# Both feed-forwards of an encoder layer by one level of Strassen's scheme

## The chip, the cores and the metric

The kernel runs on one core of a Trainium2 chip. What counts is the time of one launch on the device in microseconds, the median of several runs. PE is TensorE (matmuls), DVE is VectorE, ACT is ScalarE, POOL is GpSimd, SP is the engine whose queue issues most DMAs here.

## The reference

One layer of a bidirectional encoder on 512 tokens of width 1024, all in float32. The feed-forward width is 2816.

```
x = x + 0.5 * swiglu(rms_norm(x, ffn1_norm), w_gate1, w_up1, w_down1)
proj = rms_norm(x, mix_norm) @ w_in            # 1024 -> 2304
oa = differential attention, 8 heads, relative bias;  ob = grouped-query attention, rotary
x = x + concat(oa, ob) @ w_out                 # 1024 -> 1024
x = x + 0.5 * swiglu(rms_norm(x, ffn2_norm), w_gate2, w_up2, w_down2)
return rms_norm(x, final_norm)

swiglu(x, g, u, d) = (silu(x @ g) * (x @ u)) @ d
rms_norm(x, g)     = x * rsqrt(mean(x * x) + 1e-6) * g
```

## The kernel before

Every float32 matrix is held as two parts: a high part, the value cast to the type that PE takes (fp32r), and a low part, the value less the high part. A product is three matmuls, high by high, high by low and low by high (`mm3`, lines 180 to 183). ACT makes the high part (line 108), DVE then subtracts it from the raw value (line 109); both inputs of that subtraction lie in SBUF.

The weights come as blocks of up to 1 MB in a fixed list (`specs`). `Blocks.get` (line 116) hands out block i and has the conversion of block i + 1 and the load of block i + 2 written ahead of the products, at a higher priority. There are two raw buffers, two for high and two for low parts. All loads go through SP's queue.

x is kept transposed, features by tokens, as eight tiles `xT` of 128 by 512. `gained` (line 270) multiplies by the norm's gain and splits; the norm's factor of each token, R, is applied to the results of the products instead (lines 311 and 321). `stats` sums squares, on POOL for both feed-forwards (line 242), and `finish_stats` makes R from the sum.

`gate_up` (line 298) walks over 11 pairs of weight blocks of 256 hidden features, one of the gate and one of up. Each block makes two PSUM banks, each 8 x 3 matmuls of 512 columns (tokens), with the weights stationary. DVE multiplies by R, ACT applies silu, DVE multiplies gate by up, and the result is split into high and low again (`gT`). The first down projection (lines 402 to 417) has four passes of 256 output features, each over 22 groups of 128 hidden features, 512 tokens wide; the second (lines 920 to 942) has tokens in the rows and two passes of 512 output features.

Attention and the projections lie between; their order is set by loops over (head, 128 tokens) units with projection work filled in. The order on each engine is made by a scheduler when the program is built, from the order of writing, priorities and a model of times. The weights' conversions, the evacuations of PSUM and the splits share DVE's and ACT's queues, and each engine works its queue in order.

Of the kernel before, what the change touches and what calls it, by code (L numbers as in the profile page):

```python
# [17 lines left out]
P = 128  # L18
S = 512
# [8 lines left out]
POOL_ACC = ("f1", "f2")  # L28
SQ = 1
# [4 lines left out]
PX = "BBC"  # L34
UP = "DD"
DN1 = ("BB", "DD")
DN2 = ("AADD", "BBBC")
# [4 lines left out]
LAG_V = 4  # L42

# [31 lines left out]
class Blocks:  # L75


    def __init__(self, tc, pool, specs, ahead):
        self.tc, self.nc, self.pool, self.specs, self.ahead = tc, tc.nc, pool, specs, ahead
        self.raw, self.split = {}, {}  # L80
        self.nload = self.nsplit = 0

    def load(self, upto):
        while self.nload < min(upto, len(self.specs)):
            i = self.nload
            name, src, n, w, parts = self.specs[i]
            t = self.pool.tile([P, n, w], F32, tag="raw", name=f"raw_{name}", bufs=2)
            step = (n + parts - 1) // parts
            for a in range(0, n, step):
                b = min(n, a + step)  # L90
                for c0, c1, s in src:
                    self.nc.sync.dma_start(out=t[:, a:b, c0:c1], in_=s[:, a:b, :])
            self.raw[i] = t
            self.nload += 1

    def convert(self, upto):
        while self.nsplit < min(upto, len(self.specs)):
            i = self.nsplit
# [26 lines left out]
def build(ctx, tc, a, out):  # L125
# [13 lines left out]
    wpool = ctx.enter_context(tc.tile_pool(name="wpool", bufs=2))  # L139
    psum = ctx.enter_context(tc.tile_pool(name="psum", bufs=1, space=PS))  # L140
# [56 lines left out]
    gp = tc.tile_pool(name="ffn1", bufs=1)  # L197
    fpool = gp.__enter__()
# [759 lines left out]
```

## Time and profile before

| what | value |
|---|---|
| median of 3 runs | 1023.11 us (1021.55 to 1024.03) |
| the profiled execution | 1023.65 us, span 1021.8 us |
| mean granted TensorE clock | 0.993 |
| PE busy | 1001.2 us (98%), 4963 matmuls |
| DVE busy | 540.5 us (53%) |
| ACT busy | 395.5 us (39%) |
| POOL busy | 120.3 us (12%) |
| DMA | 105.21 MB, 103 GB/s on the mean |

The span runs from the first to the last instruction. Busy time of PE is modelled from overlapping matmuls, so a busy PE is not PE at its peak; the distance between starts tells what a matmul costs. "Idle before" is the time in which an engine stood still ahead of an instruction, and the name behind the arrow is what ended it. Times in the stages are microseconds from the span's start.

### The profile page before, as it was taken

The page shows a single profiled execution, that of the slowest core. Times are in us where ns is not written, and L with a number is a line of the kernel's source. Part 1 is how long each engine was busy: PE and PEld are TensorE (multiplying, and loading weights), DVE is VectorE, ACT ScalarE, POOL GpSimd, SP SyncE. Part 2 cuts the span into 40 slices and gives each one's busy share as a digit, 9 for nine tenths or more (in the row PEclk, how much of TensorE's full clock was granted, in tenths as well). Part 3 has the DMA queues.
Part 4 walks back from the last instruction along what each step waited for, and adds up shares of the span by engine and source line. Part 5 has one row for each costly group of instructions (what it writes and reads, how often), then busy time and mean ns, then how long its engine had stood idle before and what let it go on. Part 6 is the DMA issues. An engine that isn't in the chain of part 4 may idle for free.

```text
span 1021.8 us, 12710 instructions
## 1 busy us (share of the span) xinstructions
PE 1001.2 (98%) x4963; PEld 843.5 (83%) x4963; DVE 540.5 (53%) x898; ACT 395.5 (39%) x668; POOL 120.3 (12%) x147
## 2 busy tenths in 40 slices
PE   8999999999999999999998999999999999999997
PEld 6788888888888889899987887888888888888885
DVE  4464454444234344768996896754454444441413
ACT  6342232232223233566776565632322322311312
POOL 2100000000000000123564344400000000000000
PEclk9999999999999999999998999999999999999999
DMA  8463223223232344544322130223224223322212
GB/s 243 155 202 120 87 83 120 87 85 112 83 113 73 113 130 120 159 133 125 112 71 62 37 98 12 83 84 123 83 84 122 83 88 119 103 83 101 85 62 82
DMA packets 94224, 105.21 MB, mean 103 GB/s; under 512 B 4716, under 2 KB 78980, under 8 KB 94164
## 3 DMA queue, kind: packets, MB, share of 16 engines
q1 hardware_dynamic: 93588, 103.35, 32.8%
q8 instruction: 39, 0.64, 0.3%
q10 hardware_dynamic: 576, 1.05, 0.3%
q14 instruction: 21, 0.17, 0.1%
HBM read 93.86 MB, written 6.32 MB: 98 GB/s over the span
## 4 chain that ended last, share of the span: by engine, by line
PE 92%; DVE 3%; issue 2%; ACT 1%; DMA 1%; POOL 1%; SPq 0%; POOLq 0%; ACTq 0%; DVEq 0%
PE g L182 8%; PE g L181 8%; PE u L181 8%; PE g L183 8%; PE u L183 8%; PE u L182 8%; PE dn L183 8%; PE dn L182 8%; PE dn L181 8%; PE poA L544 2%; PE pqk L182 1%; PE pqk L181 1%; PE pqk L183 1%; PE po L181 1%; PE po L183 1%
## 5 line engine op out<-in xcount | busy, mean ns | idle before, releaser
L108 ACT CAST hi_b<-raw_b 128x1024 fp32r<-128x1024 f32 (+1 forms) x162 | 158.9, 1029 | 326.6 <-PE dn L183 82.3
L109 DVE TENSOR_TENSOR lo_b<-raw_b,hi_b 128x1024 fp32r<-128x1024 f32 (+1 forms) x162 | 192.1, 1222 | 163.0 <-ACT hi_b L108 162.8
L182 PE MATMUL g<-xl_f,hi_b 128*128 128x512 f32 x352 | 137.7, 392 | 0.0
L181 PE MATMUL u<-xh_f,hi_b 128*128 128x512 f32 x352 | 137.2, 390 | 0.0
L183 PE MATMUL g<-xh_f,lo_b 128*128 128x512 f32 x352 | 137.1, 390 | 0.0
L182 PE MATMUL u<-xl_f,hi_b 128*128 128x512 f32 x352 | 137.0, 389 | 0.0
L181 PE MATMUL g<-xh_f,hi_b 128*128 128x512 f32 x352 | 136.9, 392 | 0.0
L183 PE MATMUL u<-xh_f,lo_b 128*128 128x512 f32 x352 | 136.9, 389 | 0.0
L311 DVE TENSOR_TENSOR g<-g,R_f 128x512 f32<-128x512 f32 x44 | 30.2, 690 | 109.1 <-PE g L183 105.6
L321 DVE TENSOR_TENSOR u<-u,R_f 128x512 f32<-128x512 f32 x44 | 30.2, 690 | 91.6 <-PE u L183 91.6
L182 PEld LDWEIGHTS g<-xl_f,hi_b 128*128 128x128 f32 x352 | 66.4, 189 | 13.9 <-issue 0.2
L181 PEld LDWEIGHTS g<-xh_f,hi_b 128*128 128x128 f32 x352 | 66.3, 189 | 13.8
L183 PEld LDWEIGHTS u<-xh_f,lo_b 128*128 128x128 f32 x352 | 66.1, 188 | 14.1 <-issue 0.5
L183 PEld LDWEIGHTS g<-xh_f,lo_b 128*128 128x128 f32 x352 | 66.4, 189 | 13.6
L181 PEld LDWEIGHTS u<-xh_f,hi_b 128*128 128x128 f32 x352 | 66.1, 188 | 13.9 <-issue 0.2
L182 PEld LDWEIGHTS u<-xl_f,hi_b 128*128 128x128 f32 x352 | 66.1, 188 | 13.6
L593 ACT ACTIVATE s_A<-s_A,m_A 128x512 f32<-128x512 f32 x64 | 46.4, 726 | 30.5 <-DVE m_A L591 27.1
L312 ACT ACTIVATE g<-g 128x512 f32<-128x512 f32 x44 | 27.6, 630 | 69.4 <-DVE g L311 69.2
L591 DVE CUSTOM_DVE_ANT_0 s_A<-sA,T 128x512 f32<-128x512 f32 x64 | 43.7, 684 | 11.1 <-PE sA L589 10.1
L283 ACT CAST gT_0h<-u 128x512 fp32r<-128x512 f32 x22 | 13.7, 621 | 90.5 <-DVE u L322 90.5
L911 POOL TENSOR_TENSOR fr<-fr,mhalf 128x1 f32<-128x1 f32 x4 | 2.2, 556 | 347.1 <-DVE fr L910 347.1
L255 POOL TENSOR_TENSOR r_mx<-r_mx,mhalf 128x4 f32<-128x4 f32 x1 | 1.0, 1017 | 347.4 <-DVE r_mx L254 347.4
(273 smaller groups left out, 1976.1 us busy)
## 6 DMA issues: line engine op xcount, KB each, us to landing
raw_b<-ffn_w_up SPq DMA_DIRECT2D x22, 1024.0 KB, 5.4
raw_b<-ffn_w_gate SPq DMA_DIRECT2D x21, 1024.0 KB, 5.4
raw_b<-ffn_w_down SPq DMA_DIRECT2D x18, 1024.0 KB, 5.1
raw_b<-w_in SPq DMA_DIRECT2D x5, 1024.0 KB
toep<-nbd SPq DMA_DIRECT2D x8, 512.0 KB, 10.8
raw_b<-w_in SPq DMA_DIRECT2D x8, 512.0 KB, 4.6
raw_b<-w_out SPq DMA_DIRECT2D x4, 1024.0 KB, 5.2
T<-toep SPq DMA_DIRECT2D x8, 448.0 KB, 3.4
```

The lines of the kernel that those rows point to most:

```text
L108: self.nc.scalar.copy(out=hi[:, a:b, :], in_=t[:, a:b, :])
L109: self.nc.vector.tensor_sub(lo[:, a:b, :], t[:, a:b, :], hi[:, a:b, :].bitcast(F32))
L181: nc.tensor.matmul(ps, lh, rh, start=start, stop=False)
L182: nc.tensor.matmul(ps, lh, rl, start=False, stop=False)
L183: nc.tensor.matmul(ps, ll, rh, start=False, stop=stop)
L283: nc.scalar.copy(out=hi, in_=src)
L311: nc.vector.tensor_mul(g1, ps, R)
L312: nc.scalar.activation(g1, g1, AF.Silu)
L321: nc.vector.tensor_mul(u, ps, R)
L544: nc.tensor.matmul(ps, pt_sb[:, P * j:P * j + P], v(j), start=j == 0, stop=j == NT - 1)
L591: nc.vector.tensor_tensor_reduce(out=sc, in0=ps, in1=T[:, 384 - P * qt:896 - P * qt], scale=1.0, scalar=BIG, op0=ALU.add, op1=ALU.min, acc ...
L593: nc.scalar.activation(sc, sc, AF.Exp, bias=m[:, s:s + 1], scale=-1.0, accum_out=l1[:, qt, h:h + 1] if s == 0 else l2)
```

## The change

Each of the three products of a feed-forward is cut into 2 by 2 blocks and done with seven block products instead of eight (Winograd's form of Strassen's scheme). The blocks of the operands are added and subtracted first, and the results are put together from seven products:

- left operand: S1 = A21 + A22, S2 = S1 - A11, S3 = A11 - A21, S4 = A12 - S2
- right operand: T1 = B12 - B11, T2 = B22 - T1, T3 = B22 - B12, T4 = B21 - T2 (up to the sign)
- products: A11 B11, A12 B21, S4 B22, A22 T4, S1 T1, S2 T2, S3 T3

For gate and up the left operand is x: its token halves by its feature halves, made once for a feed-forward, from the normed x. The right operand is a weight block of 1024 by 256: POOL makes T1 to T4, ACT and DVE split all seven operands, and PE does 7 x 4 x 3 matmuls of 256 columns, half of the tokens. DVE adds the products up out of PSUM, silu follows, and H = 0.5 * silu(gate) * up stays in float32, unsplit. For down, hidden values are the left operand, 11 steps of 256 hidden features; PSUM has no room for seven accumulators, so there are three passes over H: four products at a time ("da"), then two ("db"), then one ("dc"), with 24, 12 and 6 matmuls of 512 columns a step. POOL makes the differences of the weights and of H.

x is kept natural, tokens by features (`xn`), and the norm is applied ahead of the products: squares on ACT, the root on POOL, one multiplication by factor and gain on DVE, then transposes. So R, `stats` and `finish_stats` go. The output projection is turned accordingly. Norm and transposes of tokens 256 to 511 after the first feed-forward are written ahead of the pass dc, those of tokens 0 to 255 behind it.

The diff, cut to its core:

```diff
+    def parts(self, hi, lo, src):
+        self.nc.scalar.copy(out=hi, in_=src)
+        self.nc.vector.tensor_sub(lo, src, hi.bitcast(F32))
...
+    def gate_up(self, t, shape, name):
+        sub = self.nc.gpsimd.tensor_sub
+        b11, b12, b21, b22 = t[:, 0:4, 0:P], t[:, 0:4, P:], t[:, 4:8, 0:P], t[:, 4:8, P:]
+        hi, lo = self.pair(shape, name)
+        T = {}
+        for n, x, y in ((3, b22, b12), (1, b12, b11), (2, b22, b12), (4, b21, None)):
+            if n != 1:
+                T[n] = self.fpool.tile([P, 4, P], F32, tag="T", name=f"T{n}_{name}", bufs=3)
+            sub(b12 if n == 1 else T[n], x, T[2] if n == 4 else y)
...
+        self.parts(hi[:, 4:8, :], lo[:, 4:8, :], t[:, 4:8, :])
+        self.parts(hi[:, 0:4, :], lo[:, 0:4, :], t[:, 0:4, :])
+        for p, n in ((7, 3), (6, 2), (4, 4)):
+            h, l = (self.fpool.tile([P, 4, P], F32R, tag=f"t{w}", name=f"t{w}{n}_{name}", bufs=4) for w in "hl")
+            self.parts(h, l, T[n])
...
+    def down_a(self, t, shape, name):
...
+        sub(T3, t[:, 2, :], t[:, 1, :])
+        self.nc.vector.tensor_sub(t[:, 1, :], t[:, 1, :], t[:, 0, :])
+        sub(T2, t[:, 2, :], t[:, 1, :])
+        self.parts(hi[:, 0:2, :], lo[:, 0:2, :], t[:, 0:2, :])
+        self.parts(hi[:, 3, :], lo[:, 3, :], T3)
+        self.parts(hi[:, 2, :], lo[:, 2, :], T2)
...
+    def down_b(self, t, shape, name):
...
+            self.nc.gpsimd.tensor_sub(T4, t[:, e, :], T2)
+            self.parts(hi[:, shape[0] + e, :], lo[:, shape[0] + e, :], T4)
...
+    def normed(t, G, tag):
...
+        for h in range(2):
+            squares(ss, z, t, h)
+        r = rsqrt(ss, f"{tag}{t}")
+        nc.vector.scalar_tensor_tensor(out=z, in0=xn[t], scalar=r, in1=G, op0=ALU.mult, op1=ALU.mult)
...
+    def one_block(i, j, m, L, Hj, g1, n):
...
+            for k in range(4):
+                mm3(ps, wh[:, k, :], wl[:, k, :], xh[:, k, :], xl[:, k, :], start=k == 0, stop=k == 3)
...
+        nc.vector.tensor_add(dst[:, 0::3, :], b_, p1.to_broadcast([P, 2, 256]))
...
+        nc.vector.tensor_add(dst[:, 1:3, :], c_, dst[:, 3:4, :].to_broadcast([P, 2, 256]))
+        nc.vector.tensor_add(dst[:, 3, :], c_[:, 0, :], dst[:, 2, :])
...
+        nc.vector.tensor_add(dst[:, 1:3, :], d_, dst[:, 1:3, :])
+        if m == "g":
+            nc.scalar.activation(g1, g1, AF.Silu)
         else:
...
+            nc.vector.scalar_tensor_tensor(out=Hj, in0=dst, scalar=0.5, in1=g1, op0=ALU.mult, op1=ALU.mult)
...
+        def left_a(j):
+            h = H[j]
...
+                nc.gpsimd.tensor_add(S13[:, 0, :], h[:, 2, :], h[:, 3, :])
+                nc.gpsimd.tensor_sub(S13[:, 1, :], h[:, 0, :], h[:, 2, :])
+                nc.gpsimd.tensor_sub(h[:, 2, :], S13[:, 0, :], h[:, 0, :])
+                parts(hl, slice(0, 1), h[:, 0:1, :])
+                parts(hl, slice(1, 2), h[:, 2:3, :])
+                parts(hl, slice(2, 4), S13)
...
+        get_a = ahead(left_a)
+        for j in range(NJ):
+            wh, wl = blocks.get(at[("da", i, j)])
+            hl = get_a(j)
+            for c, l, w in (("a", 0, 0), ("d", 3, 3), ("c", 2, 1), ("b", 1, 2)):
+                product(c, [x_[:, l, :] for x_ in hl], wh[:, w, :], wl[:, w, :], j == 0, j == NJ - 1)
...
+            nc.gpsimd.tensor_add(lo[:, :512], lo[:, :512], p1[:, e, :])
+            nc.gpsimd.tensor_add(hi[:, :512], hi[:, :512], u3[:, e, :])
```

`left_b` splits the other two quarters of H, 512 wide; `left_c` has POOL subtract two quarters, 256 wide, and splits the result; `ahead` has step j + 1 written with step j.

What stands in a row now, at three places. First DVE in gate/up of the first feed-forward: `g1` and `u` are the results of gate and up, `gT` the hidden values, `lo_b` a weight's low part, here for one gate and one up block before:

```order
L311 TENSOR_TENSOR g1_0_5_0_1057<-g0_5_0_1032,R_f1_375 128x512
L311 TENSOR_TENSOR g1_0_5_1_1085<-g0_5_1_1060,R_f1_375 128x512
L109 TENSOR_TENSOR lo_b12_1089<-raw_b12_1030,hi_b12_1088 128x1024 x2
L321 TENSOR_TENSOR u_0_5_0_1121<-u0_5_0_1096,R_f1_375 128x512
L322 TENSOR_TENSOR u_0_5_0_1121<-g1_0_5_0_1057,u_0_5_0_1121 128x512
L284 TENSOR_TENSOR gT0_5_0l_1125<-u_0_5_0_1121,gT0_5_0h_1124 128x512
L321 TENSOR_TENSOR u_0_5_1_1153<-u0_5_1_1128,R_f1_375 128x512
L322 TENSOR_TENSOR u_0_5_1_1153<-g1_0_5_1_1085,u_0_5_1_1153 128x512
L109 TENSOR_TENSOR lo_b13_1161<-raw_b13_1094,hi_b13_1160 128x1024 x2
L284 TENSOR_TENSOR gT0_5_1l_1157<-u_0_5_1_1153,gT0_5_1h_1156 128x512
```

and after, for one block ("u03" and "g04" are weight blocks, `tl2` to `tl4` low parts of the T differences, `utu` and `g1` the sums of products, `bg0`, `cg0`, `dg0`, `du0` PSUM banks):

```order
L418 TENSOR_TENSOR utu0_2_1034<-du0_2_1063,utu0_2_1034 128x512
L101 TENSOR_TENSOR lo_u03_1093<-raw_u03_992,hi_u03_1092 128x1024
L101 TENSOR_TENSOR tl3_u03_1106<-T3_u03_1094,th3_u03_1105 128x512
L422 SCALAR_TENSOR_TENSOR H0_2_843<-utu0_2_1034,g1_0_2_844 128x1024
L411 TENSOR_TENSOR g1_0_3_1091<-bg0_3_1134,p1g0_3_1132 128x2x256
L101 TENSOR_TENSOR tl2_u03_1110<-T2_u03_1097,th2_u03_1109 128x512
L414 TENSOR_TENSOR g1_0_3_1091<-cg0_3_1160,g1_0_3_1091 128x512
L101 TENSOR_TENSOR tl4_u03_1114<-T4_u03_1099,th4_u03_1113 128x512
L415 TENSOR_TENSOR g1_0_3_1091<-cg0_3_1160,g1_0_3_1091 128x256
L101 TENSOR_TENSOR lo_g04_1215<-raw_g04_1117,hi_g04_1214 128x1024
L418 TENSOR_TENSOR g1_0_3_1091<-dg0_3_1187,g1_0_3_1091 128x512
L101 TENSOR_TENSOR lo_g04_1215<-raw_g04_1117,hi_g04_1214 128x1024
```

The products by R and the split of the hidden values have gone; three low parts of T and four additions out of PSUM stand between the low parts of the weights.

Second POOL in the same stretch. Before, its last sums of squares and the root for R, then the root for the next norm and the first attention work:

```order
L242 TENSOR_TENSOR acc_f1_142<-acc_f1_142,sq_f16_219 128x512
L242 TENSOR_TENSOR acc_f1_142<-acc_f1_142,sq_f17_232 128x512
L255 TENSOR_TENSOR r_f1_361<-r_f1_361,mhalf_80 128x4
L255 TENSOR_TENSOR r_mx_2585<-r_mx_2585,mhalf_80 128x4
L608 TENSOR_TENSOR l2_A0_0_2788<-l2_A0_0_2788,l1_0_2786 128x1
```

and after, two weight blocks of the 22:

```order
L131 TENSOR_TENSOR T3_g04_1216<-raw_g04_1117 128x512
L131 TENSOR_TENSOR raw_g04_1117<-raw_g04_1117 128x4x128
L131 TENSOR_TENSOR T2_g04_1219<-raw_g04_1117 128x512
L131 TENSOR_TENSOR T4_g04_1221<-raw_g04_1117,T2_g04_1219 128x512
L131 TENSOR_TENSOR T3_u04_1341<-raw_u04_1239 128x512
L131 TENSOR_TENSOR raw_u04_1239<-raw_u04_1239 128x4x128
L131 TENSOR_TENSOR T2_u04_1344<-raw_u04_1239 128x512
L131 TENSOR_TENSOR T4_u04_1346<-raw_u04_1239,T2_u04_1344 128x512
```

Where POOL had no row between the two roots, there are four subtractions for each weight block now, all between SBUF tiles.

Third, the down stage. DVE before, in the passes of the first feed-forward (`xT` is x, `xl_mx` the low part for the next norm, `acc_mx` its sum of squares):

```order
L109 TENSOR_TENSOR lo_b26_2017<-raw_b26_1960,hi_b26_2016 128x1024 x2
L276 SCALAR_TENSOR_TENSOR xl_mx1_2008<-xT1_124,gcol_97,xh_mx1_2007 128x512
L242 TENSOR_TENSOR acc_mx_2004<-acc_mx_2004,sq_mx1_2011 128x512
L109 TENSOR_TENSOR lo_b27_2073<-raw_b27_2022,hi_b27_2072 128x768 x2
L109 TENSOR_TENSOR lo_b28_2129<-raw_b28_2078,hi_b28_2128 128x1024 x2
L414 SCALAR_TENSOR_TENSOR xT2_125<-dn1_0_2014,xT2_125 128x512
L276 SCALAR_TENSOR_TENSOR xl_mx2_2174<-xT2_125,gcol_97,xh_mx2_2173 128x512
L242 TENSOR_TENSOR acc_mx_2004<-acc_mx_2004,sq_mx2_2177 128x512
```

and after, in the pass da (`la06l` and `la07l` are low parts of the left operand for steps 6 and 7):

```order
L101 TENSOR_TENSOR lo_da0_6_3334<-raw_da0_6_3294,hi_da0_6_3333 128x1024
L152 TENSOR_TENSOR raw_da0_7_3346<-raw_da0_7_3346 128x512
L101 TENSOR_TENSOR lo_da0_6_3334<-T3_da0_6_3335,hi_da0_6_3333 128x512
L101 TENSOR_TENSOR lo_da0_6_3334<-T2_da0_6_3336,hi_da0_6_3333 128x512
L441 TENSOR_TENSOR la07l_3402<-S13_07_3400,la07h_3401 128x512
L441 TENSOR_TENSOR la07l_3402<-H0_7_2078,la07h_3401 128x256
L101 TENSOR_TENSOR lo_da0_7_3386<-raw_da0_7_3346,hi_da0_7_3385 128x1024
L101 TENSOR_TENSOR lo_da0_7_3386<-T3_da0_7_3387,hi_da0_7_3385 128x512
L101 TENSOR_TENSOR lo_da0_7_3386<-T2_da0_6_3336,hi_da0_7_3385 128x512
L152 TENSOR_TENSOR raw_da0_8_3397<-raw_da0_8_3397 128x512
L441 TENSOR_TENSOR la08l_3454<-H0_8_2325,la08h_3453 128x256 x2
```

and POOL there, which had no row in the stage before:

```order
L448 TENSOR_TENSOR S13_06_3349<-H0_6_1831 128x256
L449 TENSOR_TENSOR S13_06_3349<-H0_6_1831 128x256
L151 TENSOR_TENSOR T3_da0_6_3335<-raw_da0_6_3294 128x512
L450 TENSOR_TENSOR H0_6_1831<-S13_06_3349,H0_6_1831 128x256
L153 TENSOR_TENSOR T2_da0_6_3336<-raw_da0_6_3294 128x512
L151 TENSOR_TENSOR T3_da0_7_3387<-raw_da0_7_3346 128x512
L448 TENSOR_TENSOR S13_07_3400<-H0_7_2078 128x256
L449 TENSOR_TENSOR S13_07_3400<-H0_7_2078 128x256
L450 TENSOR_TENSOR H0_7_2078<-S13_07_3400,H0_7_2078 128x256
L153 TENSOR_TENSOR T2_da0_6_3336<-raw_da0_7_3346 128x512
```

On DVE a step has one 1024-wide, four 512-wide and two 256-wide instructions, none of them out of PSUM; on POOL two 512-wide and three 256-wide.

## Rows read from the trace of the kernel before

**Rows 1.** The page: busy time by engine, and the chain that ended last, by engine.

```profile
PE 1001.2 (98%) x4963; PEld 843.5 (83%) x4963; DVE 540.5 (53%) x898; ACT 395.5 (39%) x668; POOL 120.3 (12%) x147
...
PE 92%; DVE 3%; issue 2%; ACT 1%; DMA 1%; POOL 1%; SPq 0%; POOLq 0%; ACTq 0%; DVEq 0%
```

**Rows 2.** Windows by stage: us; busy us (instructions) by engine; clock; DMA share, GB/s.

```profile
0.00:18.30 18.30, 14.00 (x53) 11.07 (x54) 6.99 (x14) 10.70 (x16) 2.41 (x8) 1.00 0.98 284
18.30:257.60 239.30, 239.30 (x1060) 196.53 (x1059) 116.88 (x156) 77.25 (x102) 8.82 (x7) 1.00 0.36 116
257.60:377.40 119.80, 119.80 (x530) 99.18 (x530) 41.52 (x47) 31.34 (x40) 0.00 (x0) 1.00 0.32 99
377.40:651.70 274.30, 264.65 (x1703) 235.74 (x1702) 215.22 (x481) 172.12 (x374) 99.98 (x124) 0.98 0.33 93
651.70:653.60 1.90, 1.90 (x10) 1.59 (x9) 1.90 (x4) 1.90 (x3) 0.09 (x1) 1.00 0.74 246
653.60:893.00 239.40, 239.40 (x1068) 198.47 (x1067) 115.08 (x140) 74.12 (x96) 6.83 (x5) 1.00 0.32 99
893.00:1015.20 122.20, 122.17 (x550) 100.95 (x548) 40.78 (x55) 26.61 (x39) 1.65 (x3) 1.00 0.24 78
1015.20:1021.80 6.60, 0.00 (x0) 0.00 (x0) 2.18 (x5) 1.45 (x3) 0.54 (x1) 0.68 0.39 147
```

**Rows 3.** Timeline, PE, gate/up: start us, duration us, instruction (512 columns).

```profile
252.20 0.39 PE L181 MATMUL u<-xh_f,hi_b 128*128 128x512 f32 x1
252.43 0.39 PE L182 MATMUL u<-xl_f,hi_b 128*128 128x512 f32 x1
```

**Rows 4.** Timeline, PE, input projection: two neighbours of 256 columns.

```profile
389.47 0.28 PE L181 MATMUL pva<-hi_b,xh_mx 128*128 128x256 f32 x1
389.59 0.28 PE L182 MATMUL pva<-lo_b,xh_mx 128*128 128x256 f32 x1
```

**Rows 5.** Groups by form: count, busy us, mean ns, then idle before (DVE, POOL, ACT).

```profile
L109 DVE TENSOR_TENSOR lo_b<-raw_b,hi_b 128x1024 fp32r<-128x1024 f32 x150 | 182.2, 1250 | 118.5 <-ACT hi_b L108 118.3
L284 DVE TENSOR_TENSOR gT_0l<-u,gT_0h 128x512 fp32r<-128x512 f32 x22 | 15.2, 691 | 13.1 <-ACT gT_0h L283 13.1
L503 DVE TENSOR_TENSOR ry_q<-ry_q,rq_q 128x256 f32<-128x256 f32 x8 | 3.3, 415 | 0.0
...
L611 POOL TENSOR_TENSOR pm_A<-pm_A,s_A 128x512 f32<-128x512 f32 x16 | 22.0, 1375 | 14.0 <-DVE pm_A L610 8.9 <-DVE l_A L603 1.9 <-PE sA L589 1.1
L500 POOL TENSOR_TENSOR rq_q<-ry_q,sg_q 128x128 f32<-128x128 f32 x16 | 9.0, 585 | 6.1 <-DVE l_A L603 4.0 <-DVE of L631 1.7 <-DVE rf_q L495 0.4
...
L108 ACT CAST hi_b<-raw_b 128x1024 fp32r<-128x1024 f32 x150 | 150.3, 1050 | 277.4 <-PE u L182 77.6 <-PE g L182 73.1 <-PE dn L183 64.6
```

**Rows 6.** Timeline of DVE, then POOL, 532 to 537 us.

```profile
532.71 1.22 DVE L109 TENSOR_TENSOR lo_b<-raw_b,hi_b 128x1024 fp32r<-128x1024 f32 x1
...
534.46 1.69 DVE L109 TENSOR_TENSOR lo_b<-raw_b,hi_b 128x1024 fp32r<-128x1024 f32 x1
...
532.94 2.12 POOL L611 TENSOR_TENSOR pm_A<-pm_A,s_A 128x512 f32<-128x512 f32 x1 [0.68 <-PE po L183]
```

**Rows 7.** Timeline of DVE, then POOL, 466 to 468 us.

```profile
466.95 0.68 DVE L444 TENSOR_TENSOR yqk<-pqk,R_mx 128x512 f32<-128x512 f32 x1
...
466.46 1.30 POOL L611 TENSOR_TENSOR pm_A<-pm_A,s_A 128x512 f32<-128x512 f32 x1 [1.18 <-DVE pm_A L610]
```

**Rows 8.** Windows around the fall of the granted clock in attention.

```profile
530.00:536.30 6.30, 4.66 (x27) 3.27 (x25) 6.05 (x15) 5.90 (x14) 4.31 (x6) 1.00 0.00 0
536.30:539.80 3.50, 3.50 (x17) 3.19 (x16) 3.33 (x10) 2.35 (x6) 1.56 (x3) 0.51 0.73 182
```

[...]

**Rows 10.** The page, DMA issues: count, KB each, median us to landing.

```profile
raw_b<-ffn_w_up SPq DMA_DIRECT2D x22, 1024.0 KB, 5.4
```

More of the change, by code (lines that the diff above doesn't have):

```diff
@@ L42 @@
 LAG_V = 4
+NJ = NF // 2
+NXG = 14
 NAMES = [
@@ L418, in build, with gain_rows @@
-    gp.__exit__(None, None, None)
+    xn = [keep.tile([P, D], F32, name=f"xn{t}") for t in range(NT)]
+    def gain_rows(src):
+        g = fpool.tile([P, D], F32, tag="ut", name="G", bufs=1)
+        nc.sync.dma_start(out=g, in_=src.partition_broadcast(P))
+        return g
+    nc.sync.dma_start(out=xn[0], in_=xv[:, 0, :])
+    G = gain_rows(a["ffn1_norm"][0])
+    nc.sync.dma_start(out=xn[1], in_=xv[:, 1, :])
+    blocks.load(1)
+    for t in (2, 3):
+        nc.sync.dma_start(out=xn[t], in_=xv[:, t, :])
@@ new lines, in build, with gate_up @@
+    OPERAND = {1: "A11", 2: "A12", 3: "S4", 4: "A22", 5: "S1", 6: "S2", 7: "S3"}
+    def gate_up(i, L, between):
+        H = []
+        n = 0
+        for j in range(NJ):
+            Hj = fpool.tile([P, 4, 256], F32, tag="H", name=f"H{i}_{j}", bufs=NJ)
+            g1 = fpool.tile([P, 4, 256], F32, tag="g1", name=f"g1_{i}_{j}", bufs=2)
+            runs = []
+            for m in "gu":
+                runs.append(one_block(i, j, m, L, Hj, g1, n))
+                n += 1
+            if j == 0:
+                for r in runs:
+                    next(r)
+                between()
+            for r in runs:
+                for _ in r:
+                    pass
+            H.append(Hj)
+        return H
@@ L461, in proj_N @@
         whi, wlo = blocks.get(at[nm])
-        for t2 in range(2):
+        for t2 in (1, 0):
             ps = bank(tag, f"p{nm}{t2}")
@@ L700, in B_pv @@
         if h == 1:
-            OT[4 + pair] = split(st["pb"], st["o", "B"], "ot", f"otB{pair}", 8)
+            hi, lo = (st["pb"].tile([P, S], F32R, tag="ot", name=f"otB{pair}{w}", bufs=8) for w in "hl")
+            blocks.parts(hi, lo, st["o", "B"])
+            OT[4 + pair] = hi, lo
     def weights_T(u):
@@ L833, in build @@
             head = 2 * v["pair"] + v["h"]
-            need(lambda: len(k2) == 2 and (head // 4, 3) in qn)
+            need(lambda: len(k2) == 2 and all((head // 4, t) in qn for t in range(NT)))
             B_heads(head)
@@ L946, with late2 @@
+    def late2(G):
+        for e in range(2):
+            finish(2 + e, G)
+    down(1, H, a["final_norm"], late2, finish)
+    ffn_cm.__exit__(None, None, None)
 def kernel(**inputs):
```

700 lines of the change are left out of this document (351 added, 349 removed).

## The prediction

> **What bounds the kernel now.** Read the busy shares and the chain first: PE is busy 98% of the span and holds 92% of the chain that ended last [rows 1]. Then the table by stage: in the four feed-forward stretches, 720.7 of 1021.8 us together, PE never stops, while DVE works 49% of the gate/up stretches and a third of the down ones, and POOL does next to nothing there [rows 2]. A microsecond that PE saves there is a microsecond off the end, as long as DVE, ACT and POOL can take what they get for it. The price of a matmul is the distance between starts, since their durations overlap: 227 ns with 512 columns [rows 3], 120 ns with 256 [rows 4]. Check: a gate or up block is 48 matmuls, 48 x 0.227 = 10.9 us, and 22 of them are the 239.4 us of a gate/up stretch; 528 x 0.227 = 119.9 us is a down stretch. The profiled execution took 1023.65 us, 1.85 more than its span and 0.5 more than the median of the three runs, which nothing here hangs on.
>
> **What PE gains.** A block becomes seven products of 4 x 3 matmuls with 256 columns: 84 x 0.120 = 10.08 us for 10.88, or 221.8 us for 239.4. Down keeps 512 columns and has 11 x (24 + 12 + 6) = 462 matmuls: 104.9 us for 119.9. Both feed-forwards: 65 us less, if PE stays the bound. It is less than an eighth since 256 columns cost over half of 512: the fixed part, 120 - 107 = 13 ns, is paid twice. [...]
>
> **What DVE and POOL get.** Before, POOL has no work in gate/up and down; now it makes the differences of the weight blocks and of the hidden values, and DVE has more low parts to make. The decisive row pair is [rows 6]: DVE's low-part subtraction, both inputs in SBUF, runs 532.71 to 533.93. POOL's addition starts at 532.94 and takes 2.12 us where its fellows take 1.3 to 1.4 [rows 5]: it ends 1.13 us after DVE did. DVE's next one starts at 534.46, takes 1.69 and ends 1.09 us after POOL did. They do not run at the same time; a pair costs 1.09 + 1.13. A DVE instruction that reads PSUM is not held: one lies wholly inside a POOL addition, both at their usual length [rows 7]. So POOL's time and DVE's two-SBUF time add up, and in the changed kernel nearly all of either is of these kinds.
>
> Prices, tight (from [rows 6], smaller widths in proportion) and loose (whole means of [rows 5]): DVE 1024 wide 1.09 to 1.25 us, 512 wide 0.55 to 0.69, 256 wide 0.30 to 0.41; POOL 512 wide 1.13 to 1.375, 256 wide 0.57 to 0.85 (a third of the way from the 128-wide row to the 512-wide). I take values a little under the middle, since [rows 6] are this very pair but are one meeting only. [...]
>
> *Gate/up block.* DVE: two 1024-wide, three 512-wide, and the product of gate and up (1024) in every second block; POOL: four 512-wide. Together 8.9 tight, 10.7 loose, against PE's 10.08. DVE's four additions out of PSUM (2.1 us) can lie beside POOL. So PE just stays the bound, with little left for waits: 10.3 us a block (10.1 to 10.9), 226.6 us for 22.
>
> *Down, first pass* (11 steps of four products, 24 matmuls, 5.45 us of PE). DVE: one 1024, four 512, two 256 wide; POOL: two 512 and three 256. Together 7.9 tight, 10.1 loose, I take 8.9: over PE's time at either end. 11 x 8.9 = 98 us. ACT's share, some 3.6 us a step by its 1.05 us for 1024 [rows 5], is hidden. The weights are no bound either: 768 KB in 8.9 us is under the 116 GB/s that gate/up moves now [rows 2], and 1 MB lands 5.4 us after issue [rows 10], with two raw buffers.
>
> *Second pass* (5.5 pairs of steps, 5.45 us of PE each): one 1024, four 512 on DVE, two 512 on POOL: 5.55 to 6.8, I take 6.0: 33 us. *Between them* eight 512-wide additions into x on POOL: 9.6 us (9 to 11), in its queue among the second pass's differences, so these wait. *Third pass*: five 1024, one 512, eleven 256 on DVE and eleven 256 on POOL: 15.6 to 20.8, I take 17.5.
>
> Sum of down: 158 us; the first step is prepared during the last gate/up block (-8.9: the buffers of its operands come free only there), and PE has some 4 us left after the last conversion: 153 us (136 to 175) for 119.8.
>
> *Starts.* The norm now stands ahead of the products. Read back from the stage's end, gate/up started at 18.3 us (257.6 - 22 x 10.88). Now the queue for DVE and POOL holds, before the first two blocks can end, four 1024-wide norms, ten 512-wide DVE and four POOL steps for the sums S1 to S4, and two blocks' operands: 4.4 + 6 + 4.8 + 18.6 = 34 us. It starts at about 8 us (x's first tile and the gains, 1 MB at 284 GB/s [rows 2], then squares and the root): the pair ends near 43 us, an effective start at 23 (21 to 27). In the second feed-forward the same queue starts some 3 us before the output projection ends: 10 us (6 to 14), where 1.9 stood.
>
> *The rest.* Attention, 274.3 us: the scaling by R goes, on engines that do not end it; the norm of tiles 0 and 1 after down is some eight steps of 0.4 to 1.2 us, covered by 48 matmuls x 0.12 = 5.8 us of tiles 2 and 3: 3 us over (0 to 6). I take 277. The tail, 6.6 us, gets two 1024-wide steps for two tiles at once: 8.6.
>
> Sum: 23 + 226.6 + 153 + 277 + 10 + 226.6 + 153 + 8.6 = 1077.8, + 1.85 = **1080 us**. All ends tight: 1027; all loose: 1163.
>
> **The rivals.**
>
> *PE stays the bound, and it is faster.* The place is the first pass of down; the mechanism is that POOL's instructions fall into moments when DVE waits for ACT's high parts, or that the exclusion of [rows 6] is not general. It decides where DVE's and POOL's time of a step, overlapped, gets under 5.45 us; break-even with now is about 6.3 us a step. Then 23 + 221.8 + 104.9 + 277 + 10 + 221.8 + 104.9 + 8.6 + 1.85 = 974 us. For it: POOL and DVE are idle in down now, and prepared work could run ahead. Against: 7.9 us of exclusive time in 5.45 even at the tight end, and only two buffers of weights to run ahead with.
>
> [...]
>
> *Gate/up is bound by DVE and POOL too.* POOL's differences lie in three T buffers that DVE frees one by one; if the additions out of PSUM find no POOL instruction beside them, a block is 9.8 + 2.1 = 11.9 us: + 1.6 x 44 = + 70, 1150 us. For it: both engines work in order. Against: DVE's order has a PSUM addition behind nearly each of the T conversions.
>
> That the change does not do what it says is out: the built order has the 84 and 42 matmuls.
>
> **How the numbers follow.** Forecast 0.68, clock 0.12, gate/up bound 0.08, PE-bound 0.12. Under 0.3% (3 us) a measurement cannot tell from no change; a small part of the PE-bound case (0.03, partial overlap) ends there. Faster 0.09, same 0.03, slower 0.88. The range leaves the PE-bound case out below and most of the third rival above, and holds the forecast's tight to loose ends and the clock case: 1032 to 1145.
>
> **What will show it.** By stage: gate/up of 222 to 240 us with PE over 93% busy; down near 153 us with PE near 70% and DVE, its blocked time counted, near 100%. The low-part subtractions of 512 in down should take far more than 0.69 us on the mean, and POOL's differences more than 1.375; PSUM additions should keep 0.68. Matmuls of 256 columns should start 120 ns apart. It is wrong if down takes about 105 us with PE full, or if both engines show their undisturbed lengths while overlapping; wrong in size if the starts cost less than 4 or more than 15 us each.

## The result, and the profile after

The changed kernel takes 1114.76 us (median of four runs, 1113.46 to 1116.41); the kernel before took 1023.14 us in the same session. The ratio is 1.0898, 95% interval 1.0875 to 1.0921: slower by 92 us. The forecast was 1080 us, with a range from 1032 to 1145. The profiled execution took 1113.46 us, 1.86 more than its span of 1111.6.

The page answers [rows 1]: PE, 98% busy before, is 89% busy now; DVE has gone from 53% to 84%, POOL from 12% to 57%.

```profile
PE 984.9 (89%) x6415; PEld 884.8 (80%) x6415; DVE 934.9 (84%) x1270; ACT 548.8 (49%) x999; POOL 635.7 (57%) x496
```

The table by stage answers [rows 2], with the same columns. In order: the first start and gate/up, the three passes of down, attention, the second start and gate/up, and the three passes again.

```profile
0.00:42.95 42.95, 24.11 (x101) 19.66 (x102) 32.34 (x39) 22.95 (x46) 29.20 (x24) 0.68 0.49 162
42.95:259.70 216.75, 216.06 (x1790) 214.67 (x1789) 198.84 (x228) 103.38 (x146) 144.42 (x84) 1.00 0.38 121
259.70:349.10 89.40, 70.08 (x267) 50.87 (x265) 79.88 (x75) 35.63 (x65) 66.67 (x55) 0.92 0.30 94
349.10:389.80 40.70, 34.74 (x133) 27.22 (x132) 36.98 (x35) 18.42 (x29) 26.84 (x17) 0.87 0.26 86
389.80:423.90 34.10, 21.50 (x84) 17.74 (x84) 20.09 (x37) 15.37 (x35) 7.83 (x11) 0.80 0.28 85
423.90:704.40 280.50, 268.04 (x1705) 236.29 (x1703) 207.93 (x474) 166.09 (x372) 97.30 (x125) 0.98 0.33 95
704.40:739.30 34.90, 18.58 (x96) 16.36 (x95) 30.99 (x34) 20.33 (x43) 21.69 (x15) 0.71 0.19 61
739.30:953.50 214.20, 214.20 (x1785) 214.20 (x1786) 190.77 (x211) 101.12 (x145) 133.61 (x83) 1.00 0.32 100
953.50:1044.60 91.10, 69.02 (x267) 50.16 (x266) 80.18 (x77) 35.70 (x65) 67.32 (x56) 0.94 0.28 92
1044.60:1085.50 40.90, 33.13 (x133) 25.55 (x133) 39.28 (x41) 19.64 (x35) 31.45 (x23) 0.96 0.22 66
1085.50:1101.30 15.80, 15.30 (x67) 12.12 (x65) 13.26 (x21) 7.63 (x17) 8.33 (x6) 1.00 0.42 152
```

Two neighbours of PE in gate/up, 256 columns each, answer [rows 3, 4]: they start 0.12 us apart.

```profile
65.80 0.28 PE L252 MATMUL dg<-S4f1h,lo_g 128*128 128x256 f32 x1
65.92 0.28 PE L250 MATMUL dg<-A22f1h,th_g 128*128 128x256 f32 x1
```

PE is full only in the two gate/up stretches. In the first pass of down DVE is busy for 80 of 90 us and POOL for 67. Read from these bounds, with a start counted as the end of gate/up less 22 x 10.08 us, the terms of the forecast are:

| term | forecast | measured | off by |
|---|---|---|---|
| first start | 23 | 37.9 | +14.9 |
| gate/up, each | 226.6 | 221.8 | -4.8 |
| first down | 153 | 164.2 | +11.2 |
| attention | 277 | 280.5 | +3.5 |
| second start | 10 | 27.3 | +17.3 |
| second down | 153 | 147.8 | -5.2 |
| tail | 8.6 | 10.3 | +1.7 |

They sum to 1111.6 us, against the forecast's 1077.8. The starts are 32 of the 34 us between them; the other terms cancel nearly. The start is defined by 10.08 us a block; read directly, the 20 blocks behind the first pair took 202.5 us in the first stretch (57.3 to 259.8) and 201.6 in the second (752.1 to 953.7), 10.13 and 10.08 us each.

The middle of the first pass shows why it takes longer than PE needs. First the window that lies inside it, then DVE's and POOL's timelines (start, duration, instruction, in brackets what ended the wait).

```profile
281.00:343.00 62.00, 50.02 (x198) 35.30 (x196) 62.00 (x55) 27.98 (x50) 50.67 (x38) 1.00 0.31 101
```

```profile
304.45 1.22 DVE L152 TENSOR_TENSOR raw_da<-raw_da 128x512 f32<-128x512 f32 x1
305.59 1.83 DVE L441 TENSOR_TENSOR la06l<-H,la06h 128x256 fp32r<-128x256 f32 x2
307.34 1.78 DVE L441 TENSOR_TENSOR la06l<-S,la06h 128x512 fp32r<-128x512 f32 x1
...
320.49 1.22 DVE L152 TENSOR_TENSOR raw_da<-raw_da 128x512 f32<-128x512 f32 x1
```

```profile
305.81 1.32 POOL L153 TENSOR_TENSOR T_da<-raw_da 128x512 f32<-128x512 f32 x1 [0.69 <-DVE raw_da L152]
307.10 1.47 POOL L151 TENSOR_TENSOR T_da<-raw_da 128x512 f32<-128x512 f32 x1
309.27 0.77 POOL L448 TENSOR_TENSOR S<-H 128x256 f32<-128x256 f32 x1 [0.69 <-DVE la06l L441]
```

DVE has no idle moment in 62 us. The low part `la06l`, 512 wide, takes 1.78 us where its like took 0.69 [rows 5]; POOL's T difference beside it takes 1.47. From one L152 to the same one two steps later are 16.04 us, 8.02 a step; PE needs 5.45. For the first passes of both feed-forwards together, DVE's low parts of the T differences take 1.25 us on the mean and POOL's differences 1.47 and 1.58, while additions out of PSUM in gate/up keep their 0.68, as the forecast's signs had it:

```profile
L101 DVE TENSOR_TENSOR lo_da<-T_da,hi_da 128x512 fp32r<-128x512 f32 x44 | 53.7, 1252 | 0.0
```

### The profile page after: what moved, and what is told of

Its sections match the earlier page's. It is cut to its first block, busy times and chain, and to the rows that moved or that the text cites. A ratio compares the mean times of both kernels' runs of the same rounds, so it can differ in the third digit from the quotient of the medians.

```text
span 1111.6 us, 17270 instructions
## 1 busy us (share of the span) xinstructions
PE 984.9 (89%) x6415; PEld 884.8 (80%) x6415; DVE 934.9 (84%) x1270; ACT 548.8 (49%) x999; POOL 635.7 (57%) x496
## 5 line engine op out<-in xcount | busy, mean ns | idle before, releaser
L131 POOL TENSOR_TENSOR T_g<-raw_g 128x512 f32<-128x512 f32 x44 | 79.2, 1800 | 76.5 <-DVE tl_u L101 57.5
L131 POOL TENSOR_TENSOR T_u<-raw_u 128x512 f32<-128x512 f32 x44 | 65.6, 1492 | 57.7 <-DVE tl_g L101 54.1
L100 ACT CAST th_u<-T_u 128x512 fp32r<-128x512 f32 x66 | 40.9, 620 | 95.4 <-PE cg L251 44.7
L101 DVE TENSOR_TENSOR lo_g<-raw_g,hi_g 128x1024 fp32r<-128x1024 f32 x44 | 73.8, 1676 | 5.4 <-ACT hi_g L100 5.4
L101 DVE TENSOR_TENSOR lo_u<-raw_u,hi_u 128x1024 fp32r<-128x1024 f32 x44 | 71.8, 1635 | 4.9 <-ACT hi_u L100 4.8
L101 DVE TENSOR_TENSOR tl_u<-T_u,th_u 128x512 fp32r<-128x512 f32 x66 | 70.1, 1063 | 0.0
L101 DVE TENSOR_TENSOR tl_g<-T_g,th_g 128x512 fp32r<-128x512 f32 x66 | 64.5, 980 | 0.2 <-ACT th_g L100 0.2
L100 ACT CAST hi_u<-raw_u 128x1024 fp32r<-128x1024 f32 x44 | 44.7, 1047 | 30.1 <-PE du L251 12.3
L100 ACT CAST hi_g<-raw_g 128x1024 fp32r<-128x1024 f32 x44 | 44.7, 1049 | 28.5 <-PE dg L251 15.4
L101 DVE TENSOR_TENSOR lo_da<-T_da,hi_da 128x512 fp32r<-128x512 f32 x44 | 53.7, 1252 | 0.0
L151 POOL TENSOR_TENSOR T_da<-raw_da 128x512 f32<-128x512 f32 x22 | 34.8, 1584 | 27.6 <-DMA raw_da<-ffn_w_down 20.6
L153 POOL TENSOR_TENSOR T_da<-raw_da 128x512 f32<-128x512 f32 x22 | 32.3, 1470 | 12.4 <-DVE raw_da L152 7.3
```

Source lines behind the costliest of these rows:

```text
L100: self.nc.scalar.copy(out=hi, in_=src)
L101: self.nc.vector.tensor_sub(lo, src, hi.bitcast(F32))
L131: sub(b12 if n == 1 else T[n], x, T[2] if n == 4 else y)
L151: sub(T3, t[:, 2, :], t[:, 1, :])
L153: sub(T2, t[:, 2, :], t[:, 1, :])
```

## Experiments: what holds the first down pass

**POOL's sums left out of the first pass.** In `down_a` and `left_a` (cut; the products take plain quarters instead, and the second pass's T4 is made from these):

```
-        sub(T3, t[:, 2, :], t[:, 1, :])
-        sub(T2, t[:, 2, :], t[:, 1, :])
-                nc.gpsimd.tensor_add(S13[:, 0, :], h[:, 2, :], h[:, 3, :])
-                nc.gpsimd.tensor_sub(S13[:, 1, :], h[:, 0, :], h[:, 2, :])
-                nc.gpsimd.tensor_sub(h[:, 2, :], S13[:, 0, :], h[:, 0, :])
```

> In the first down pass of both feed-forwards POOL's five sums a step are left out (the products take plain quarters in their place, so the output is another); DVE's, ACT's and PE's instructions stay in number and width. Theory: with POOL silent DVE needs 1.14 + 4 x 0.60 + 2 x 0.33 = 4.2 us a step, PE is the bound with 24 x 0.227 = 5.45 us, the pass takes 60 us and some 6 for its start where it took 84; the 512-wide low parts go back from 1.25-1.43 to 0.68 us; total about 1080 us (1070 to 1090). Rival (weights arriving, ACT's high parts or the two buffers bound the pass): within 5 us of 1115.

Measured: 1057.12 us. The pass takes 61.7 us, in both feed-forwards, and a step 5.45; the groups show DVE's low parts at their undisturbed length and DVE waiting for weights. First the window of the pass, then two groups of DVE:

```profile
261.20:322.90 61.70, 60.34 (x268) 49.60 (x267) 45.73 (x68) 29.69 (x53) 5.33 (x5) 1.00 0.42 135
```

```profile
L101 DVE TENSOR_TENSOR lo_da<-raw_da,hi_da 128x512 fp32r<-128x512 f32 x17 | 11.1, 684 | 0.0
L146 DVE TENSOR_TENSOR raw_da<-raw_da 128x512 f32<-128x512 f32 x7 | 4.8, 691 | 6.5 <-DMA raw_da<-ffn_w_down 6.5
```

The rival falls: with POOL silent, PE is the bound. The total fell more than expected, since I had measured the old pass to its last start of a step (84 us) and not to its last matmul (89.4 and 91.1): 27.7 + 29.4 = 57 us, and 1114.8 - 57 = 1058. This edit also takes away what DVE waits for from POOL; the run below that prices the meeting by itself has no such waits.

**All sums on DVE.** Thirteen lines of this kind, in both feed-forwards:

```
-        sub = self.nc.gpsimd.tensor_sub
+        sub = self.nc.vector.tensor_sub
```

> All block differences and sums of both feed-forwards go from POOL to DVE; the products are untouched. Theory (DVE instructions with two SBUF inputs and POOL instructions keep each other out, so that their times add up): a 512-wide sum costs 0.60 us from start to start on DVE where it held the pair for 1.13 on POOL, so although DVE gets more work, a step of the first down pass falls from 8.0 to 4.2 + 2 x 0.60 + 3 x 0.33 = 6.4 us; gate/up stays at 10.08 us a block; the starts lose some 4 to 6 us each. Total about 1058 us (1045 to 1075). Rival (the two engines run side by side and DVE's instructions are long for another reason): DVE is 90% busy already and gets five more instructions a step at the 0.95 to 1.25 us that such ones now take, 13 us a step, total near 1230 us.

Measured: 1067.88 us, ratio to the kernel before 1.0425 (1.0407 to 1.0442), 47 us faster than the change, with DVE doing all of POOL's sums besides its own work. The profiled execution took 1073.28 us. The first window is the first pass, the second gate/up:

```profile
255.00:329.00 74.00, 64.96 (x269) 50.17 (x267) 73.17 (x135) 38.08 (x66) 0.00 (x0) 0.95 0.35 108
45.00:255.00 210.00, 210.00 (x1748) 209.41 (x1748) 194.43 (x295) 98.90 (x141) 0.00 (x0) 1.00 0.39 124
```

The pass falls from 89.4 to 74.0 us, 6.7 a step, near the 6.4 worked out, with DVE full; gate/up stays full on PE. The starts fell by 4.5 and 2.2 us, the second less than expected. POOL's help made the pass longer: what it took off DVE's hands it took twice in time (a 512-wide sum alone is 1.22 us on POOL and 0.61 on DVE, priced below).

**The meeting priced by itself.** Ten instructions of 512 columns on one or two engines at a time; the inputs are the same SBUF tile (or one PSUM bank):

> Not the reference's computation: ten stages of ten 512-wide float instructions on one or two engines at once, to price the meeting itself. Theory: a two-input SBUF subtraction takes about 0.60 us from start to start on DVE and 1.25 on POOL alone; both together take the sum, 18 us for ten of each, not the 12.5 of the slower one. A DVE subtraction with one input in PSUM beside POOL takes 12.5. ACT beside either takes the time of the slower. Open: whether a DVE instruction with one SBUF input, or a POOL instruction with one or none, meets in the same way. Rival (only bandwidth is shared, or the slow-down comes from the kernel's buffers): together 12.5 to 14 us in every stage.

The timelines of DVE, POOL and ACT merge each stage into one row: start, duration of the ten. The tile names tell the stage: `v` DVE alone, `g` POOL alone, `vg` both with two SBUF inputs, `pg` DVE with one input from PSUM, `og` DVE with one SBUF input (times a constant), `vo` POOL with one, `vm` POOL only writing, `sg` and `vs` with ACT.

```profile
4.68 6.10 DVE L45 TENSOR_TENSOR d_v<-J_start 128x512 f32<-128x512 f32 x10
25.48 15.70 DVE L45 TENSOR_TENSOR d_vg<-J_g__108 128x512 f32<-128x512 f32 x10 [14.69 <-ACT J_g__108 L81]
43.50 6.07 DVE L47 TENSOR_TENSOR d_pg<-bank,J_vg__151 128x512 f32<-128x512 f32 x10 [2.32 <-ACT J_vg__151 L81]
57.07 13.03 DVE L49 TENSOR_SCALAR d_og<-J_pg__194 128x512 f32<-128x512 f32 x10 [7.50 <-ACT J_pg__194 L81]
89.92 8.17 DVE L45 TENSOR_TENSOR d_vo<-J_tg__280 128x512 f32<-128x512 f32 x10 [2.32 <-ACT J_tg__280 L81]
106.91 6.11 DVE L45 TENSOR_TENSOR d_vm<-J_vo__323 128x512 f32<-128x512 f32 x10 [8.81 <-ACT J_vo__323 L81]
...
12.03 12.24 POOL L58 TENSOR_TENSOR g_g<-J_v__85 128x512 f32<-128x512 f32 x10 [11.59 <-ACT J_v__85 L81]
25.59 16.70 POOL L58 TENSOR_TENSOR g_vg<-J_g__108 128x512 f32<-128x512 f32 x10 [1.32 <-ACT J_g__108 L81]
43.61 12.26 POOL L58 TENSOR_TENSOR g_pg<-J_vg__151 128x512 f32<-128x512 f32 x10 [1.31 <-ACT J_vg__151 L81]
105.65 4.72 POOL L62 MEMSET g_vm<- 128x512 f32 x10
113.82 12.28 POOL L58 TENSOR_TENSOR g_sg<-J_vm__366 128x512 f32<-128x512 f32 x10 [3.45 <-ACT J_vm__366 L81]
...
113.70 5.30 ACT L67 COPY s_sg<-J_vm__366 128x512 f32<-128x512 f32 x10
```

Alone, DVE needs 6.10 us and POOL 12.24. Together they need 16.70: 1.67 a pair, nine tenths of the sum of 1.83, and the 0.55 + 1.13 = 1.68 of the forecast's tight prices. With one of DVE's inputs in PSUM neither is longer (6.07 and 12.26). POOL that only writes does not lengthen DVE (6.11, beside it for 3.5 us), and POOL beside ACT's copies keeps its time (12.28; ten of the copies take 5.30, beside POOL as beside DVE). A DVE instruction with one SBUF input is held too (ten take 13.03; one like it, `yf` of the kernel before, takes 0.49 us), and POOL with one input lengthens DVE from 6.10 to 8.17. The rival falls: shared bandwidth alone would have made it 12.5 to 14 us by its own terms, and here neither engine waits for a buffer of the other.

## Experiments: the third pass, and the parts of the change apart

In the first feed-forward the third pass took 34.1 us, in the second 15.8. Three rows around it, of PE, ACT and PE:

```profile
397.50 3.65 PE L314 MATMUL xt_mx<-ident,z_mx 128*128 128x128 f32 x16 [7.60 <-DVE z_mx L304]
...
405.68 0.41 ACT L440 CAST lc00h<-S 128x256 fp32r<-128x256 f32 x1
...
406.14 0.80 PE L250 MATMUL dc<-hi_dc,lc00h 128*128 128x512 f32 x1 [5.00 <-ACT lc00h L440]
```

PE waits 7.6 us for the norm of tiles 2 and 3, and then 5.0 for the pass's first operand, which stands behind that norm's conversions on ACT. So the order was tried in which the norm comes within the pass:

```
-        late(G)
         for j in range(NJ):
             hl = get_c(j)
+            if j == 6:
+                late(G)
```

> The norm of token tiles 2 and 3 stands in the code within the third down pass (ahead of its step 6) and not ahead of it. Theory (PE's 16 us without products between 390 and 406 us come from the order: its transposes wait for the norm, and the third pass's operands stand behind the norm's conversions on ACT): PE ends the first feed-forward's down stage near 408 to 412 us and not at 424, total about 1102 us (1098 to 1108). Rival (the third pass is bound by DVE and POOL, as the forecast had it, or the wait only moves to the next norm): less than 3 us off 1115.

Measured: 1114.34 us, no gain, as the rival had it. Products of the third pass now run from 391.2, but the pass ends at 419.0, since PE does va products in between, and then PE waits 5.2 us for the next norm, until 425.2. The kernel is 4.0 us ahead after that (the middle score matmul of group A starts at 526.5 for 530.5) and loses it at once. The same window of attention, first of the changed kernel, then with this edit (the clock is the third number from the end):

```profile
520.00:560.00 40.00, 35.83 (x253) 32.79 (x252) 33.37 (x102) 28.52 (x72) 16.67 (x28) 0.91 0.44 133
```

```profile
520.00:560.00 40.00, 36.32 (x212) 32.77 (x211) 31.81 (x94) 26.24 (x68) 15.49 (x25) 0.74 0.37 106
```

At 0.74 instead of 0.91 PE gets through 212 matmuls instead of 253 while it is as busy (36.3 and 35.8 us): it is slower there, and does not wait more. So the hole is one of order, as the theory had it, but closing it moved most of it to the next norm, and the lower granted clock (0.74 for 0.91 in these 40 us) took the rest. What lowered it is open, and this is one execution of each.

**Plain down.** Gate/up by seven products, down by plain products (528 matmuls, H split 1024 wide); the core of the edit, cut:

```
-            add(("da", i, j), f"da{i}_{j}", "down_a", [3, 512], ...
+            add(("dn", i, j), f"dn{i}_{j}", "plain", [2, 1024], [(full, d[:, 2 * j:2 * j + 2, :])])
```

> One part of the change alone: gate/up by seven products as in the changed kernel, down by plain products (528 matmuls of 512 columns a feed-forward, H split 1024 wide one step ahead, all eight PSUM banks, the last two steps by token tile). Theory (the down part costs what the 164 and 148 us of the changed kernel show against 120 plain; gate/up gains and the starts lose as they stand): down about 122 us in both feed-forwards with PE full, some 6 us more at the hand-over to attention, total about 1050 us (1040 to 1062), still slower than the kernel before by the starts. Rival (x kept natural with the norm ahead of the products is what makes down slow, by its hand-over): above 1080 us.

Measured: 1045.32 us, ratio 1.021 (1.0187 to 1.0233), as the theory had it. Down is full on PE:

```profile
260.70:382.40 121.70, 121.70 (x548) 100.96 (x548) 42.83 (x48) 31.59 (x43) 1.65 (x3) 1.00 0.27 91
```

So the seven-product down costs 69 of the 92 us lost, and what is left of it another 22: the starts (38.9 and 28.3 us here) are 47 us longer than before, the gate/up blocks 35 us shorter, and attention with the norm ahead of it 9 us longer (283.1 us).

**The same with the sums on DVE.**

> Plain down and the gate/up sums on DVE, nothing else. Theory: gate/up stays at 10.08 us a block; the starts lose the 5 and 2 us that they lost when all sums went to DVE: 1038 us (1033 to 1043) for 1045. Rival (with POOL silent DVE is the bound of gate/up, 9.2 us and more of work a block with waits): 1050 us or more.

Measured: 1036.62 us, ratio 1.0117 (1.0095 to 1.014). The theory holds, and nothing points to DVE as the bound of gate/up: the run is 8.7 us faster for carrying all of gate/up's sums on DVE, and with all sums there, above, PE was busy 210.00 of 210.00 us of gate/up.

## Experiments: the starts

In the first start the norm itself waits for the meeting of the two engines. The rows are DVE, POOL, POOL, DVE, all but the T difference for token tile 3:

```profile
24.43 0.14 DVE L293 TENSOR_SCALAR r_f<-r_f 128x1 f32<-128x1 f32 x1
...
24.65 3.40 POOL L131 TENSOR_TENSOR T_u<-raw_u 128x512 f32<-128x512 f32 x1 [1.50 <-DVE r_f L293]
28.01 0.55 POOL L294 TENSOR_TENSOR r_f<-r_f,mhalf 128x1 f32<-128x1 f32 x1
...
28.59 2.29 DVE L304 SCALAR_TENSOR_TENSOR z_f<-xn,r_f,G 128x1024 f32<-128x1024 f32 x1 [1.69 <-POOL r_f L294]
```

The root for tile 3 has its input at 24.6 and is begun at 28.0, behind a T difference that takes 3.4 us, while DVE makes three low parts without a stop from 24.5 to 26.9. The last low part of S4 ends at 48.0, and then some 70 of the pair's 168 matmuls are still to do, in the second start as well: 8.4 us.

**First pair plain.** Eight plain products, token half by token half, for the first gate and up block. The core of the edit, cut; it also splits A21, which plain products need, and sets the splits of A21 and A22 ahead of the sums:

```
-                add((m, i, j), f"{m}{i}{j}", "gate_up", [NK, 256], parts)
+                add((m, i, j), f"{m}{i}{j}", "gate_up" if j else "plain", [NK, 256], parts)
```

> Only the first gate and the first up block of each feed-forward are computed by eight plain products instead of seven, token half by token half, so that they need no sums S1 to S4 and no differences of weights; 2 x 12 x 0.12 = 2.9 us of matmul more each time. Theory (the starts are long because 81 of the first 168 matmuls stand behind the last of the sums): the effective start of gate/up (its end less 22 x 10.08 us) falls from 37.9 to about 26 us and from 27 to about 15 us behind the output projection, total about 1090 us (1080 to 1098). Rival (the starts are DVE's queue itself, norm, low parts and sums, so that the next pair waits as long): less than 6 us off 1115.

Measured: 1125.01 us, ratio 1.0978 (1.0942 to 1.1014): slower. The starts grew, to 44.7 and 33 us. ACT in the second shows why:

```profile
739.58 1.28 ACT L403 ACT_TABLE_LOAD   x1 [8.00 <-PE gp L252]
740.88 0.60 ACT L403 ACTIVATE g<-gp 128x512 f32<-128x512 f32 x1
741.37 0.62 ACT L288 ACTIVATE z_f<-xn 128x512 f32<-128x512 f32 x1
```

The squares for token tile 2 (`z_f`) stand behind a SiLU that waits 8 us for the first half's 48 matmuls, so the second half's norm begins when the first half's products are done. Neither theory had this. In the first start that SiLU waits 0.4 us only; what made it longer was not taken apart. Together with plain down and the sums on DVE it cost more. In this kernel and in the two last ones below "sums on DVE" means the differences of the weights; S3 and S4 are POOL's again.

> Seven products in gate/up alone, their sums on DVE, the first pair of blocks plain, down plain: the three edits together. If their gains add up (1050 us with the plain down, less 25 us by the first pair, less 7 us of the starts by the sums on DVE), 1018 us (1005 to 1030), even with the kernel before or a little faster. Rival (DVE is the bound at the starts either way, and the gains are the same microseconds): 1035 to 1045 us.

Measured: 1060.72 us, 24 us above the kernel with plain down and all sums on DVE.

**The norm ahead of that SiLU**, by priority, with scratch of its own, and the bias tables behind the pair:

> As the kernel with the first pair of blocks plain, with three things in another order: the norm of the next token half stands ahead of the first half's SiLU and copies on ACT and DVE, its scratch tile is no longer the one that the gate's result uses, and the relative-bias tables come behind the pair. Theory (that kernel lost its gain because ACT's squares for token tile 2 stood behind a SiLU that waits for 48 matmuls, and PE's products behind the tables' matmuls): the effective start of gate/up falls from 37.9 to 24 to 28 us, that of the second feed-forward from 27 to 13 to 19 us behind the output projection; total 1080 to 1102, likeliest 1090 us. Rival (the first pair is bound by the norm, the sums and the low parts in whatever order): 1105 us or more.

Measured: 1094.01 us, 21 us under the change. The starts are 28.8 and 20.9 us: less gain in each than expected, but both fell. So they were a matter of what PE can do before the sums are there, and of order; which of the three changes of order did it was not taken apart.

**All three together**, and then with the norm of tiles 0 and 1 made while the output projection works on the others:

> Plain down, sums on DVE, first pair plain with the norm ahead. Theory: 1038 us with plain down and sums on DVE, less 10 us for each start, 1018 us (1008 to 1030), even with or faster than the kernel before. Rival (the starts stay): 1036 us or more.

Measured: 1027.78 us, ratio 1.003 (1.0018 to 1.0043); starts 28.9 and 19.1 us. The core of the next edit, cut:

```
+                    if part == 1 and hh == 1 and t < 2:
+                        with tc.high_priority(400):
+                            pre["f2", t] = normed(t, st["G2"], "f2", early=True)
```

> As the kernel with plain down, sums on DVE and a plain first pair, with two norms earlier: the gains of the second feed-forward's norm are loaded and the norms of token tiles 0 and 1 made while the output projection still works on tiles 2 and 3, ahead of the weights' differences on DVE; and tile 0's norm for attention is made while down works on tile 1. Theory (that kernel's second start is 19 us because tile 1's normed rows are there 9 us after the last output product: DVE's queue holds four differences that wait for weights, and the gains land 2.8 us after it): second start 9 to 13 us behind the output projection, total 1018 us (1013 to 1023), a little faster than the kernel before. Rival (the weights' conversions bound that start in any order): 1025 us or more.

Measured: 1023.61 us, ratio 0.9994 (0.9982 to 1.0005): no difference from the kernel before, and between the theory's range and the rival's. Tile 1's normed rows, DVE's `z_f`, first in the kernel with all three, whose output projection ends at 655.6, then in this one, where it ends at 656.5:

```profile
664.55 1.28 DVE L294 SCALAR_TENSOR_TENSOR z_f<-xn,r_f,G 128x1024 f32<-128x1024 f32 x1
```

```profile
658.82 1.28 DVE L299 SCALAR_TENSOR_TENSOR z_f<-xn,r_f,G 128x1024 f32<-128x1024 f32 x1
```

The norm came 6.6 us sooner behind the projection, but the second start fell by 4.0 only, to 15.1 us, not to 9 to 13; what holds the rest is open. The first fell to 24.7. Attention grew from 283.2 to 288.3 us, again in a stretch with a lower granted clock (0.87 for 0.96 in the 90 us around its middle; again the kernel with all three first, then this one):

```profile
480.00:570.00 90.00, 79.76 (x581) 72.06 (x579) 78.69 (x212) 63.45 (x155) 49.77 (x68) 0.96 0.29 85
```

```profile
476.00:566.00 90.00, 81.17 (x543) 73.98 (x541) 75.59 (x203) 60.60 (x149) 47.10 (x66) 0.87 0.31 89
```

No version beat the kernel before beyond the interval.

## Why the forecast was right, and where it was off

**What PE gains: right.** Matmuls of 256 columns start 0.12 us apart and a block takes 10.08 us (10.13 in the first stretch); at 10.3 the forecast was up to 4.8 us too long for each stage.

**DVE and POOL add up: right, and at the tight end.** The step of the first pass took 8.02 us, for 7.9 tight and 8.9 forecast, since the kernel meets as [rows 6] did, pair after pair. Choosing near the middle, because that row was one meeting only, cost 0.9 us a step. It does not show in the pass, 89.4 us for 98 - 8.9 = 89, because the other half of that term failed: the first step was not prepared during the last gate/up block. But for twelve matmuls, PE began the pass's products at 269.6, 9.9 us into it:

```profile
269.62 0.79 PE L250 MATMUL dd<-hi_da,la00h 128*128 128x512 f32 x1 [6.87 <-ACT la00h L440]
```

That operand comes from POOL's sums of the hidden values, which start at 267.1. They are written into the one `ut` buffer, which the last gate/up block uses until 265.1, and POOL stands at a T difference until its weights land at 265.8. So the pass came out right by two errors that cancel, which is luck. The second pass with its additions into x, 40.7 us, is the forecast's 42.6.

**The third pass: the wrong mechanism.** I priced it as DVE's and POOL's work, 17.5 us, and 4 for PE's rest. Where nothing stands in its way it is PE's own 15 us (second feed-forward, 15.8); in the first it is 34.1, by the norm's place in the queues of PE and ACT. The step that failed is that I summed two engines and did not follow the order of the code, where `late(G)` stands ahead of the pass. The two errors of this term, +13 and -6 us, half cancel.

**The starts: half of the whole error each time.** The queue for DVE and POOL was sized at 34 us from 8 us on, to end at 43; it ended at 48. Then I set the pair's end at the queue's end, as if all its matmuls lay beside it. Some 70 of 168 came after the last low part of S4 and the pair ended at 57. For the second start the same step failed: the pair ended at 752 us, where I had it near 735. Both starts lie outside the forecast's ranges for them (21 to 27 and 6 to 14 us), and they cost 19.6 and 25.4 us more than before, over the 15 at which the forecast itself said that it would be wrong in size. The total stayed in the range by the width that other terms gave it. (By its own terms the tight ends sum to 1028 and the loose ones to 1161, not to 1027 and 1163.)

**The rivals.** PE as the bound fell (it needs POOL's sums left out altogether: 61.7 us a pass). The clock case, a granted clock that falls throughout the first pass as it did for 3.5 us in attention [rows 8], did not come about: from 281 to 343 us it was 1.00 with PE busy 50 of 62 us. It fell at the pass's first wait (0.50 from 264.9 to 275.0, with matmuls of 512 columns 0.43 us apart), and around the second and third passes (0.87 and 0.80 over them). Gate/up bound by DVE and POOL fell as well: PE was busy 214.2 of 214.2 us.

## What to carry to other kernels

Before work goes to an idle engine, look for one pair of rows where it runs beside the engine it is to help: if both get longer, price the sum of the two (here 1.67 us a pair, for 0.61 and 1.22 alone), and the faster engine doing it all may be quicker (here 74.0 us a pass for 89.4). A saving per product counts after the longer start is paid; find the last operand of the first block and count the matmuls behind it (here some 70 of 168). Where one stage feeds the next, follow each engine's order through the hand-over: here a SiLU that waited 8.0 us held the squares behind it, and a norm that PE waited 7.6 us for held the third pass's first operand, 5.0 us more.

## What the chip showed that was not expected

Even an instruction of one column was held: the sum of two columns (`r_f`, L292) took 0.16 us alone and 1.21 beside a POOL difference that runs from 718.4 to 720.0.

```profile
706.90 0.16 DVE L292 TENSOR_TENSOR r_f<-ss_f 128x1 f32<-128x1 f32 x1
718.76 1.21 DVE L292 TENSOR_TENSOR r_f<-ss_f 128x1 f32<-128x1 f32 x1
```

And a gain ahead of attention was given back twice within it, 4 to 5 us each time, in stretches with a lower granted clock (0.74 for 0.91, and 0.87 for 0.96). Both were seen in one profiled execution each, and what lowered it is open.
